# Trainium2, one core: the opening loads of a two-layer hybrid decoder trunk, in pieces of 256 KB instead of 128 KB

## The chip, the core and the metric

The kernel runs on one core of a Trainium2 chip. The core's engines run beside each other and are tied by semaphores: PE (TensorE: products of 128x128 weights with a moving operand, into PSUM), ACT (ScalarE), DVE (VectorE), POOL (GpSimd) and SP (SyncE), which here issues nearly all DMAs. The metric is the device time of one execution in microseconds (us), as the median of several runs. The profile is of one further execution.

## What is computed

Two layers of a decoder trunk on 1024 tokens of width 1024, all in float32. Cut to what matters:

```python
for l in range(DEPTH):                                # 2 layers
    h = rmsnorm(x, attn_norm[l])
    proj = h @ w_in[l]                                # split among four mixers
    y_a = mla_attention(c_q, c_kv, k_r, ...)          # latent attention
    y_b = short_gated_conv(g_b, g_c, u_conv, conv_w[l])
    y_c = multiscale_pool(u_pool, pool_w[l], pool_scale[l])
    y_d = swa_sink_attention(q_sw, k_sw, v_sw, ...)   # sliding window
    mixed = rmsnorm_per_group(stack(y_a, y_b, y_c, y_d)) * mix_norm[l]
    x = x + mixed @ w_o[l]
    h2 = rmsnorm(x, ffn_norm[l])
    gate, up = split(h2 @ w_gate_up[l])
    x = x + (silu(gate) * up) @ w_down[l]
return rmsnorm(x, final_norm)
```

## The kernel before

The tokens are the free axis, in two halves t of 512; the width is cut into eight k-tiles of 128 rows. So x is sixteen tiles of 128x512 (256 KB), held transposed in DRAM (`xT`).

A float32 product is made of three passes in a reduced format: an operand f is split into a rounded high part (one ACT instruction, L377 or, with a gain, L382) and a low part, f minus the high part (one DVE instruction, L380 or L383). `split` (L373 on) does this, `mm3` (L345) issues high by high, high by low and low by high. Each product of a weight tile with a moving tile thus stands as three rows on PE.

Before anything has landed PE runs `WARM` passes on a tile of ones (L606); what they make is not used. A float32 pass shows as two records in the profile, so WARM = 6 is twelve records.

The first work is two column groups of layer 0's input projection (the sliding-window keys and values), accumulated over the eight k-tiles in two PSUM banks, `ps_mm` and `ps_s`. Their weights come ahead of all others in four pieces `w_first` of 128x512, each for two k-tiles. Per k-tile, ACT makes the high part of the x-tile and its square for the norm, DVE the low part and the sum of squares; per weight piece there is a cast on ACT and a subtraction on DVE. A further weight, `w_in[0, 0]`, follows for the queries.

In the program before, the first k-tile is entered in halves of FIRST = 256 columns (`enter_first`, L477 on, `first_weights`, L494 on): SP loads

1. `first`: the small parameters of all layers (86 columns) and the first 256 columns of the first x-tile,
2. the first half of the first weight piece (what the first k-tile needs),
3. the other 256 columns of the first x-tile,
4. the second half of the weight piece,

and then whole tiles and pieces in the order of need. The first k-tile's products run over 256 columns each, twelve in all.

Loads, ACT, DVE, PE, POOL and SP orders are not written out by hand beyond that. The program is traced, a list scheduler (`Order`, with its own table of costs) looks for an order of all instructions on each engine, chooses buffers for it, tries it against drawn delays and imposes the best one found (`scheduled_kernel`). `behind(a, b)` adds an order between two instructions without a wait. The loads at the start are chained with it, so SP keeps their sequence. A changed program is scheduled anew from its start to its end.

At most eight of SP's loads are on their way: the ninth waits for the first to land.

After the input projection come the mixers and the output projection (in the profile until about 425 us), then the FFN (until about 1040), and the same again for layer 1 (mixers until 1425). In the FFN the products follow a scheme of sums of blocks; some sums are made ahead by DMAs into DRAM tensors `gd` and loaded from there (L1387).

Of the kernel before, what the change touches and what calls it, by code (L numbers as in the profile page):

```python
# [47 lines left out]
WARM = 6  # L48
FIRST = 256
# [80 lines left out]
def trunk_kernel(ctx: ExitStack, tc: tile.TileContext, ins, out, given=None, ends=None):  # L130
# [214 lines left out]
    def mm3(o, terms, start=True, stop=True, again=False):  # L345

        nonlocal last_mm
        n, opening = len(terms), None
        for k, (wh, wl, rh, rl) in enumerate(terms):
            for i, (w, r) in enumerate(((wh, rh), (wh, rl), (wl, rh))):  # L350
                last_mm = pe.matmul(  # L351
                    o,
                    w,
                    r,
                    start=start and k == 0 and i == 0,
                    stop=stop and k == n - 1 and i == 2,
                    skip_group_check=again,
                )
                opening = opening or last_mm
        return opening  # L360
# [10 lines left out]
    last_lo = None  # L371

    def split(hi, lo, f, gain=None, after=None):  # L373

        nonlocal last_lo
        if gain is None:
            a = act.copy(hi, f)  # L377
            if after is not None:
                behind(a, after)
            last_lo = dve.tensor_tensor(out=lo, in0=f, in1=rd(hi), op=ALU.subtract)  # L380
        else:
            a = act.activation(hi, f, AF.Copy, scale=gain)  # L382
            last_lo = dve.scalar_tensor_tensor(  # L383
                out=lo, in0=f, scalar=gain, in1=rd(hi), op0=ALU.mult, op1=ALU.subtract
            )
        return a
# [80 lines left out]
    first_cols = (slice(0, FIRST), slice(FIRST, HT))  # L467
# [9 lines left out]
    def enter_first():  # L477


        s = F.pair()  # L480
        loads.append(sp.dma_start(F.ap2(s)[:, HT - PC_ALL : HT + FIRST], ins["first"]))
# [10 lines left out]
        behind(dve.tensor_copy(par, got), lows[0])  # L492

    def first_weights(n):  # L494

        ks = slice(n * 2 * P, (n + 1) * 2 * P)
        if n == 0:
            wraw.append(F.half())
            wkv.append((R.half(), R.half()))
        f, (h, lo) = F.ap(wraw[0])[:, ks], wkv[0]  # L500
        loads.append(sp.dma_start(f, ins["w_first"][0][:, ks]))
        split(R.ap(h)[:, ks], R.ap(lo)[:, ks], f)
# [10 lines left out]
    def first_terms(i, t, k, cols):  # L513
        cs = slice(2 * (k % 2) * P + i * P, 2 * (k % 2) * P + i * P + P)
        hi, lo = (R.ap(v)[:, cs] for v in wkv[k // 2])
        return [(hi, lo, *(R.ap(v)[:, cols] for v in hh[k][t]))]
# [28 lines left out]
    for l in range(L):  # L545
# [57 lines left out]
        if l == 0:  # L603
# [3 lines left out]
            wkv, wraw, loads, lows, opened = [], [], [], [], []  # L607
            for j in range(NK // 2):
                if j == 0:
                    enter_first()  # L610
                    F.free(wraw[0])
                else:
                    wraw.append(F.half())
# [12 lines left out]
            F.free(xf[0][0] - 1)  # L626
# [27 lines left out]
            for i in range(L):  # L654
                for o, c, n in ((nsink, PC_SINK, 4), (nffn, PC_FFN, NK)):
                    d = dve.tensor_scalar(
# [6 lines left out]
                    behind(d, last_lo)  # L663
# [1665 lines left out]
def _layout(i):  # L2329
# [69 lines left out]
    a["first"] = c(np.concatenate([lay.reshape(P, -1), fin, a["xT"][0, :, :FIRST]], axis=1))  # L2399
    two = a["w_in"][0, 2:4].reshape(2, P, NK // 2, 2, P)  # L2400
    a["w_first"] = c(two.transpose(2, 1, 3, 0, 4)).reshape(NK // 2, P, HT)
# [30 lines left out]
```

## Time and profile before

| what | us |
|---|---|
| median of three runs (2028.12 to 2030.2) | 2028.17 |
| the profiled execution's own time | 2027.67 |
| its span, first to last instruction | 2025.9 |
| PE busy | 2011.1 |
| DVE busy | 1533.0 |
| ACT busy | 1026.0 |

How to read it: the span is what the profile covers; the time has some launch and end around it. The rows of a timeline give start, duration, engine, line and operation, then the tile written and those read, and the count where several like ones are merged; in brackets stands how long the engine was idle before and what released it. Rows of busy time by stretch give the stretch, its length, then PE, PEld (weight loads), DVE, ACT and POOL busy with their counts, the granted TensorE clock, the share of the DMA engines' time in use and GB/s. `PEld` lies beside PE and takes no time of its own as long as PE is busy.

### The profile page before, as it was taken

Reading aid. Unit: us, or ns where it says so; the run is one execution under the profiler, and the core shown is the slowest. Engines: PE = TensorE matmul, PEld = TensorE weight load, DVE = VectorE, ACT = ScalarE, POOL = GpSimd, SP = SyncE. Lnnn points to the kernel's source line nnn. Section 1 sums busy time; section 2 is a strip of 40 time slices with the busy share of each in tenths; the row PEclk is TensorE's granted clock in tenths of the full one; section 3 lists DMA queues with packets and bytes.
Section 4 is the critical chain, followed back from the end, with each engine's and each line's share of the span. In section 5 each row is a group of like instructions: output and inputs, shape, how many; then the busy total and the mean of one; then the engine's idle time right before and its main releaser. Section 6 shows DMA issues by size and latency. Waiting matters only on the chain.

```text
span 2025.9 us, 26686 instructions
## 1 busy us (share of the span) xinstructions
PE 2011.1 (99%) x9392; PEld 1671.5 (83%) x9392; DVE 1533.0 (76%) x2332; ACT 1026.0 (51%) x1774; POOL 570.2 (28%) x440
## 2 busy tenths in 40 slices
PE   9999999999999999999999999999999999999998
PEld 7888888888888888888888888888888888888887
DVE  8889978997677778776646898789876766775554
ACT  8457657843333335545533676677433333354343
POOL 0110000047877883000000000000687677710000
PEclk9999999999999999999999999999999999999999
DMA  6552233346767677998822134242454554487552
GB/s 206 112 105 62 72 103 110 122 150 213 208 203 204 199 209 262 385 349 290 285 71 66 48 94 130 98 154 89 164 183 166 201 172 168 163 314 250 188 178 84
DMA packets 157623, 345.90 MB, mean 171 GB/s; under 512 B 15280, under 2 KB 63024, under 8 KB 157488
## 3 DMA queue, kind: packets, MB, share of 16 engines
q1 hardware_dynamic: 150768, 326.88, 47.0%
q0 software_dynamic: 6720, 17.30, 5.2%
q8 instruction: 74, 1.21, 0.2%
q14 instruction: 61, 0.50, 0.1%
HBM read 248.71 MB, written 111.67 MB: 178 GB/s over the span
## 4 chain that ended last, share of the span: by engine, by line
PE 95%; DVE 3%; ACT 1%; DMA 1%; issue 0%; SPq 0%; DVEq 0%; ACTq 0%
PE ps_mm L351 37%; PE ps_s L351 29%; PE ps_t L351 11%; PE ps_pv L351 9%; PE ps_pv L1195 2%; PE ps_t L1183 2%; PE ps_s L1125 1%; PE ps_s L1127 1%; PE ps_s L1126 1%; PE ps_pv L797 1%; PE ps_s L719 1%; PE ps_t L785 1%; PE ps_t L437 1%; PE ps_s L996 0%; DVE u L429 0%
## 5 line engine op out<-in xcount | busy, mean ns | idle before, releaser
L351 PE MATMUL ps_mm<-u,u 128*128 128x512 f32 (+1 forms) x3415 | 837.5, 388 | 2.9 <-ACT u L377 1.9
L351 PEld LDWEIGHTS ps_mm<-u,u 128*128 128x128 f32 x3415 | 624.0, 188 | 127.4 <-ACT u L377 4.5
L380 DVE TENSOR_TENSOR u<-u,u 128x1024 fp32r<-128x1024 f32 (+4 forms) x466 | 510.1, 1115 | 180.9 <-ACT u L377 151.5
L351 PE MATMUL ps_s<-u,u 128*128 128x512 f32 (+1 forms) x2607 | 620.0, 389 | 1.0 <-ACT u L382 1.0
L377 ACT CAST u<-u 128x1024 fp32r<-128x1024 f32 (+4 forms) x466 | 393.4, 862 | 378.3 <-DMA u<-ad 75.2
L351 PEld LDWEIGHTS ps_s<-u,u 128*128 128x128 f32 x2607 | 489.5, 188 | 102.7 <-ACT u L382 1.2
L351 PE MATMUL ps_t<-u,u 128*128 128x512 f32 (+1 forms) x1080 | 245.1, 377 | 0.1
L351 PEld LDWEIGHTS ps_t<-u,u 128*128 128x128 f32 x1080 | 194.9, 188 | 38.0 <-DVE u L1412 0.4
L1192 POOL MEMSET u<- 128x128 f32 x32 | 6.1, 217 | 700.2 <-PE ps_mm L351 468.3
L351 PE MATMUL ps_pv<-u,u 128*128 128x512 f32 x792 | 190.7, 389 | 0.2 <-DVE u L1444 0.2
L351 PEld LDWEIGHTS ps_pv<-u,u 128*128 128x128 f32 x792 | 148.6, 188 | 31.5 <-DVE u L1444 0.7
L1577 POOL TENSOR_TENSOR tm<-tm,u 128x512 f32<-128x512 f32 x76 | 120.9, 1591 | 130.3 <-ACT tm L1575 130.2
L1575 ACT ACTIVATE tm<-tm 128x512 f32<-128x512 f32 x76 | 48.0, 632 | 144.1 <-DVE tm L458 144.0
L377 ACT CAST u<-ps_t 128x512 fp32r<-128x512 f32 (+3 forms) x132 | 64.4, 503 | 51.5 <-PE ps_t L1183 26.5
L380 DVE TENSOR_TENSOR u<-ps_t,u 128x512 fp32r<-128x512 f32 (+3 forms) x132 | 74.8, 581 | 15.1 <-ACT u L377 14.0
L1473 ACT COPY tm<-ps_s 128x512 f32<-128x512 f32 x62 | 36.3, 586 | 96.6 <-PE ps_s L351 92.0
L1393 POOL TENSOR_TENSOR u<-u 128x512 f32<-128x512 f32 x38 | 71.3, 1876 | 33.9 <-DVE u L380 32.7
L1655 POOL TENSOR_TENSOR u<-u,u 128x352 f32<-128x352 f32 x64 | 80.4, 1257 | 1.1
L325 POOL DMA_DIRECT2D gd<-in_w_gu x36 | 32.0, 890 | 172.8 <-PE ps_t L351 72.1
L1655 POOL TENSOR_TENSOR u<-u 128x352 f32<-128x352 f32 x64 | 74.2, 1162 | 7.7 <-DMA u<-in_w_dn 7.2
L421 ACT ACTIVATE tm<-u 128x512 f32<-128x512 f32 (+1 forms) x91 | 53.9, 599 | 43.1 <-DVE u L1839 35.6
L458 DVE TENSOR_TENSOR tm<-tm,u 128x512 f32<-128x512 f32 x76 | 70.6, 929 | 2.2
(205 smaller groups left out, 2311.0 us busy)
## 6 DMA issues: line engine op xcount, KB each, us to landing
u<-in_w_gu SPq DMA_DIRECT2D x82, 512.0 KB, 3.8
ad<-u SPq DMA_DIRECT2D x154, 256.0 KB, 2.8
u<-ad SPq DMA_DIRECT2D x70, 512.0 KB, 6.1
u<-in_w_dn SPq DMA_DIRECT2D x64, 352.0 KB, 3.5
qd<-u SPq DMA_DIRECT2D x64, 352.0 KB, 2.6
u<-in_w_in SPq DMA_DIRECT2D x43, 512.0 KB, 4.8
u<-qd SPq DMA_DIRECT2D x32, 512.0 KB, 5.6
gd<-in_w_gu POOLq DMA_DIRECT2D x30, 512.0 KB, 6.8
```

The source lines that it names most:

```text
L351: last_mm = pe.matmul(o, w, r, start=start and k == 0 and i == 0, stop=stop and k == n - 1 and i == 2, skip_group_check=again,)
L377: a = act.copy(hi, f)
L380: last_lo = dve.tensor_tensor(out=lo, in0=f, in1=rd(hi), op=ALU.subtract)
L421: act.activation(q, f, AF.Square)
L458: dve.tensor_tensor(out=o, in0=a, in1=b, op=ALU.mult)
L1183: pe.transpose(p[:, b * P : (b + 1) * P], pr[b][j // 4][:, (j % 4) * P : (j % 4 + 1) * P], ident,)
L1195: pe.matmul(py[:, c0:], v_of(j, h), R.ap(s)[:, c0:], start=j == 0 and n == 0, stop=j == nj - 1 and n == 1,)
L1393: pool.tensor_tensor(out=q4, in0=q4, in1=F.ap(self.raw[1] + 1), op=ALU.add)
L1473: act.copy(o, p)
L1575: last_silu = act.activation(g, g, AF.Silu)
L1577: pool.tensor_tensor(out=g, in0=g, in1=r, op=ALU.mult)
L1655: pool.tensor_tensor(out=o, in0=a, in1=b, op=ALU.add)
```

## The change

The first k-tile is no longer entered in halves. The weight pieces are loaded whole (128x512, 256 KB), the first of them ahead of everything; the second load is the whole first x-tile with the parameters behind it (128x598, 299 KB). `first_weights`, the tracking of the last low part and the orders that hung on it (parameter copy behind the first low part, negated parameters behind the last) are gone. WARM is 8, so sixteen records on ones instead of twelve. In DRAM `first` and `w_first` are laid out to fit.

```diff
-WARM = 6
-FIRST = 256
+WARM = 8
...
         s = F.pair()
-        loads.append(sp.dma_start(F.ap2(s)[:, HT - PC_ALL : HT + FIRST], ins["first"]))
-        xf[0][0] = s + 1
-        got, f = F.ap(s)[:, HT - PC_ALL :], F.ap(s + 1)
-        h, lo = hh[0][0] = R.half(), R.half()
-        first_weights(0)
-        for n, cols in enumerate(first_cols):
-            if n:
-                loads.append(sp.dma_start(f[:, cols], x_in[0, :, cols]))
-            split(R.ap(h)[:, cols], R.ap(lo)[:, cols], f[:, cols], got[:, PC_ATTN : PC_ATTN + 1])
-            lows.append(last_lo)
-        first_weights(1)
-        behind(dve.tensor_copy(par, got), lows[0])
...
+        loads.append(sp.dma_start(F.ap2(s)[:, : HT + PC_ALL], ins["first"]))
+        xf[0][0] = s
+        got = F.ap(s + 1)[:, :PC_ALL]
+        hh[0][0] = half_split(F.ap(s), got[:, PC_ATTN : PC_ATTN + 1])
+        dve.tensor_copy(par, got)
...
             for j in range(NK // 2):
+                wraw.append(F.half())
+                loads.append(sp.dma_start(F.ap(wraw[j]), ins["w_first"][j]))
                 if j == 0:
+                    wkv.append(half_split(F.ap(wraw[0])))
+                    F.free(wraw[0])
                     enter_first()
-                    F.free(wraw[0])
                 else:
-                    wraw.append(F.half())
-                    loads.append(sp.dma_start(F.ap(wraw[j]), ins["w_first"][j]))
                     loads.append(enter_load(0, 2 * j))
...
-                    for cols in [whole] if t or k else first_cols:
-                        for i, p in enumerate(pkv[t]):
-                            m = mm3(
-                                p[:, cols], first_terms(i, t, k, cols), k == 0 and not cols.start, k == NK - 1
-                            )
-                            if cols.start:
-                                behind(m, opened[i])
-                            elif t == k == 0:
-                                opened.append(m)
+                    for i, p in enumerate(pkv[t]):
+                        mm3(p, first_terms(i, t, k), k == 0, k == NK - 1)
...
-                    d = dve.tensor_scalar(
+                    dve.tensor_scalar(
...
-                    behind(d, last_lo)
```

What this makes of the order is seen at three places, all at the program's start. First SP, the sequence of the loads (tile written, source, partitions x columns); before:

```order
L481 DMA u_112<-in_first 128x342
L501 DMA u_115<-in_w_first 128x256
L488 DMA u_112<-in_xT 128x256
L501 DMA u_115<-in_w_first 128x256
L475 DMA u_129<-in_xT 128x512
L614 DMA u_129<-in_w_first 128x512
L475 DMA u_132<-in_xT 128x512 x2
```

and SP's loads now:

```order
L585 DMA u_114<-in_w_first 128x512
L473 DMA u_119<-in_first 128x598
L467 DMA u_125<-in_xT 128x512
L585 DMA u_125<-in_w_first 128x512
L467 DMA u_128<-in_xT 128x512 x2
```

Four loads have become two; from the second x-tile on the sequence is the same.

On ACT, at the same place, L382 is an x-tile's high part, L377 a weight's, L412 and L421 are squares; before:

```order
L382 ACTIVATE u_114<-u_112 128x256
L377 CAST u_116<-u_115 128x256
L412 ACTIVATE u_159<-u_112 128x512
L377 CAST u_116<-u_115 128x256
L382 ACTIVATE u_114<-u_112 128x256
L382 ACTIVATE u_176<-u_129,par 128x512
L421 ACTIVATE tm<-u_129 128x512
L382 ACTIVATE u_191<-u_132,par 128x512
L377 CAST u_188<-u_129 128x512
```

and ACT now (the same lines are L375, L370, L405 and L414):

```order
L370 CAST u_116<-u_114 128x512
L375 ACTIVATE u_121<-u_119 128x512
L405 ACTIVATE u_155<-u_119 128x512
L414 ACTIVATE tm<-u_125 128x512
L375 ACTIVATE u_166<-u_125,par 128x512
L375 ACTIVATE u_181<-u_128,par 128x512
L370 CAST u_178<-u_125 128x512
```

The weight now comes first, the second tile's square stands ahead of its high part, and the third x-tile (its high part is u_181, before u_191) still stands ahead of the second weight piece.

On PE the first tile's rows, and where the third tile's begin (the moving operand's high or low part stands first, the weight piece second); before:

```order
L606 MATMUL ps_pv<-tm 128x128 x6
L351 MATMUL ps_mm<-u_114,u_116 128x256
L351 MATMUL ps_s<-u_114,u_116 128x256 x2
...
L351 MATMUL ps_mm<-u_176,u_116 128x512 x2
L351 MATMUL ps_s<-u_176,u_116 128x512 x2
L351 MATMUL ps_mm<-u_191,u_188 128x512
```

and PE now:

```order
L581 MATMUL ps_pv<-tm 128x128 x8
L350 MATMUL ps_s<-u_121,u_116 128x512
L350 MATMUL ps_mm<-u_121,u_116 128x512 x3
L350 MATMUL ps_s<-u_121,u_116 128x512 x2
L350 MATMUL ps_s<-u_166,u_116 128x512
L350 MATMUL ps_mm<-u_166,u_116 128x512 x3
L350 MATMUL ps_mm<-u_181,u_178 128x512
L350 MATMUL ps_s<-u_166,u_116 128x512 x2
```

The first tile has six rows for twelve, and two of the second tile's rows (u_166) have moved behind the third tile's first one (u_181). Past the start, rows have moved against each other on all engines in the mixers of both layers; on PE hardly any have in the FFN.

More of the change, by code (lines that the diff above doesn't have):

```diff
@@ L379, in split @@
                 behind(a, after)
-            last_lo = dve.tensor_tensor(out=lo, in0=f, in1=rd(hi), op=ALU.subtract)
+            dve.tensor_tensor(out=lo, in0=f, in1=rd(hi), op=ALU.subtract)
         else:
             a = act.activation(hi, f, AF.Copy, scale=gain)
-            last_lo = dve.scalar_tensor_tensor(
+            dve.scalar_tensor_tensor(
                 out=lo, in0=f, scalar=gain, in1=rd(hi), op0=ALU.mult, op1=ALU.subtract
@@ L511, in enter_sum, with first_terms @@
         F.free(xf[k][t])
-    def first_terms(i, t, k, cols):
-        cs = slice(2 * (k % 2) * P + i * P, 2 * (k % 2) * P + i * P + P)
+    def first_terms(i, t, k):
+        cs = slice(2 * i * P + k % 2 * P, 2 * i * P + k % 2 * P + P)
         hi, lo = (R.ap(v)[:, cs] for v in wkv[k // 2])
-        return [(hi, lo, *(R.ap(v)[:, cols] for v in hh[k][t]))]
+        return [(hi, lo, R.ap(hh[k][t][0]), R.ap(hh[k][t][1]))]
     def gain(d):
@@ L606, in trunk_kernel @@
                 pe.matmul(warm[:, :P], start, start, start=True, stop=True)
[L607 removed]
+            wkv, wraw, loads = [], [], []
             for j in range(NK // 2):
+                wraw.append(F.half())
+                loads.append(sp.dma_start(F.ap(wraw[j]), ins["w_first"][j]))
                 if j == 0:
+                    wkv.append(half_split(F.ap(wraw[0])))
+                    F.free(wraw[0])
                     enter_first()
[L611 removed]
                 else:
[L613 to L614 removed]
                     loads.append(enter_load(0, 2 * j))
@@ L625, in trunk_kernel @@
                 behind(a, b)
-            F.free(xf[0][0] - 1)
+            F.free(xf[0][0] + 1)
             pkv = []
@@ L2398, in _layout @@
     fin = i["final_norm"].reshape(NK, P).T
-    a["first"] = c(np.concatenate([lay.reshape(P, -1), fin, a["xT"][0, :, :FIRST]], axis=1))
-    two = a["w_in"][0, 2:4].reshape(2, P, NK // 2, 2, P)
-    a["w_first"] = c(two.transpose(2, 1, 3, 0, 4)).reshape(NK // 2, P, HT)
+    a["first"] = c(np.concatenate([a["xT"][0, :, :HT], lay.reshape(P, -1), fin], axis=1))
+    two = a["w_in"][0, 2:4].reshape(2, P, NK // 2, 2 * P)
+    a["w_first"] = c(two.transpose(2, 1, 0, 3)).reshape(NK // 2, P, HT)
     a["rope_q"], a["rope_k"], a["const"] = _constants()
```

14 lines of the change are left out of this document (1 added, 13 removed).

## The prediction

> **What bounds the kernel now.** I read the page's busy table first, then the busy time by stretch, then the order of time of the first 13 us, and last the loads' times to landing. The table:
>
> ```profile
> span 2025.9 us, 26686 instructions
> PE 2011.1 (99%) x9392; PEld 1671.5 (83%) x9392; DVE 1533.0 (76%) x2332; ACT 1026.0 (51%) x1774; POOL 570.2 (28%) x440
> ```
>
> PE is without work for 2025.9 - 2011.1 = 14.8 us in all. The change removes no product from it: twelve of 256 columns become six of 512. So only these 14.8 us can shrink, and anything lost must be added to them. Busy time by stretch (the second column is the stretch's length, the third PE's busy time) says where they lie; the last line is the page's group of most of PE's products:
>
> ```profile
> 0.00:9.84 9.84, 6.78 (x31) 5.49 (x31) 4.11 (x10) 5.84 (x11) 0.21 (x4) 1.00 0.71 225
> 11.98:25.00 13.02, 13.02 (x57) 10.79 (x58) 12.94 (x20) 12.43 (x23) 0.00 (x0) 1.00 1.04 390
> 50.00:425.00 375.00, 373.34 (x1841) 308.81 (x1840) 333.76 (x689) 241.42 (x514) 20.01 (x35) 1.00 0.38 99
> 425.00:1040.00 615.00, 615.00 (x2715) 509.13 (x2714) 441.37 (x465) 267.46 (x353) 277.46 (x200) 1.00 0.74 245
> 1040.00:1425.00 385.00, 383.97 (x1900) 320.37 (x1899) 319.54 (x670) 242.14 (x517) 5.47 (x18) 1.00 0.29 93
> 1425.00:1990.00 565.00, 565.00 (x2522) 469.00 (x2521) 377.98 (x408) 225.02 (x302) 265.30 (x182) 1.00 0.56 191
> 2016.86:2025.90 9.04, 0.53 (x2) 0.12 (x2) 3.34 (x6) 1.53 (x4) 0.00 (x0) 0.59 0.34 116
> L351 PE MATMUL ps_mm<-u,u 128*128 128x512 f32 (+1 forms) x3415 | 837.5, 388 | 2.9 <-ACT u L377 1.9
> ```
>
> Four parts: 9.84 - 6.78 = 3.06 us in the start, 1.66 in layer 0's mixers (375 - 373.34), 1.03 in layer 1's (385 - 383.97), and 9.04 - 0.53 = 8.51 at the end, where the last tiles are normalized and stored. Both FFN stretches have none, and there 615 us hold 2715 products: one each 0.227 us. A product's own record lasts 0.388 us in the mean, the next beginning before its end, so waits under some 0.16 us don't show as idle; the 2.7 us of the mixers are what can be seen. The granted clock is 1.00 until the end, so the throttle is out of it.
>
> **The start, step by step.** In order of time (start us, us, what; in brackets the idle time before and what ended it):
>
> ```profile
> 0.74 0.39 SPq L481 DMA_DIRECT2D u<-in_first  x1
> 1.19 0.42 SPq L501 DMA_DIRECT2D u<-in_w_first  x1
> 1.05 2.93 PE L606 MATMUL ps_pv<-tm 128*128 128x128 f32 x12 [1.05 <-DVE tm L200]
> 4.13 0.55 PE L351 MATMUL ps_mm<-u,u 128*128 128x256 f32 x1
> 4.83 0.28 PE L351 MATMUL ps_mm<-u,u 128*128 128x256 f32 x1
> 6.32 0.38 PE L351 MATMUL ps_s<-u,u 128*128 128x256 f32 x1 [0.97 <-ACT u L382]
> 4.93 0.63 ACT L412 ACTIVATE u<-u 128x512 f32<-128x512 f32 x1 [0.98 <-DMA u<-in_xT]
> 6.17 0.71 ACT L382 ACTIVATE u<-u,par 128x512 fp32r<-128x512 f32 x1
> 6.79 0.61 ACT L421 ACTIVATE tm<-u 128x512 f32<-128x512 f32 x1
> 6.92 0.75 DVE L383 SCALAR_TENSOR_TENSOR u<-u,par,u 128x512 fp32r<-128x512 f32 x1
> 8.55 0.72 ACT L382 ACTIVATE u<-u,par 128x512 fp32r<-128x512 f32 x1 [1.15 <-DMA u<-in_xT]
> 9.19 0.60 ACT L377 CAST u<-u 128x512 fp32r<-128x512 f32 x1
> 9.84 0.50 PE L351 MATMUL ps_mm<-u,u 128*128 128x512 f32 x1 [0.87 <-ACT u L377]
> ```
>
> PE opens with the passes on ones, has its first product at 4.13, then waits 0.97 and 0.87 us. The point that counts is 9.84: there the products of the third k-tile begin, released by the cast of the second weight piece (9.19), which stands on ACT behind the third x-tile (8.55), which waited for its DMA. From 11.98 to 25 PE is busy throughout. So the work of the first two k-tiles (twelve products of 512 columns, 12 x 0.227 = 2.7 us) lies in a hole of 9.84 - 4.13 = 5.7 us, and when exactly they begin costs nothing until the hole is used up. **The third x-tile's landing sets the start, not the first load's.**
>
> Landings (KB each, then us from issue to landing; issue times from the rows above and the SP queue's):
>
> ```profile
> 3.55 0.91 SPq L475 DMA_DIRECT2D u<-in_xT  x2
> u<-in_first SPq DMA_DIRECT2D x1, 171.0 KB, 2.4
> u<-in_w_first SPq DMA_DIRECT2D x1, 128.0 KB, 2.2
> u<-in_xT SPq DMA_DIRECT2D x1, 256.0 KB, 3.3
> u<-in_xT SPq DMA_DIRECT2D x1, 256.0 KB, 5.0
> GB/s 0 0 0 0 0 18 82 285 324 329 202 171 188 222 246 324 352 410 362 260 239 253 259 212 205 157 225 307 341 382 362 355 382 396 389 403 417 417 389 417
> ```
>
> The first load is there at 0.74 + 2.4 = 3.14, the third x-tile at 3.55 + 5.0 = 8.55. The last row is what the DMA engines moved in slices of 0.3 us of the first 12 us. It dips from 329 to about 200 GB/s between 3.0 and 4.5, while the three 128 KB pieces pass: SP issues one load each 0.45 us (1.19 - 0.74), so 128 KB pieces can't feed more than 131 KB / 0.45 us = 290 GB/s. With pieces of 256 KB and more that limit is about 580, and this dip should go.
>
> **What the change does to it.**
> 1. *The first product comes later.* It needs the weight piece (256 KB) and the whole first tile with the parameters (299 KB), together 568,000 bytes. By the slices some 115,000 have moved at 2.4 us; the rest at 325 GB/s takes 1.4 us, so 3.8; landings here lag the bytes by 0.5 us (first load: its 175,000 bytes have passed at 2.6, landed 3.14) to 1.6 us (third x-tile: passed at 6.9 by the slices, landed 8.55). So 4.3 to 5.4; I take 4.5, near the first load's lag. Then ACT's 512-column activation, 0.72, gives PE its first product at **5.25 instead of 4.13**. Its low half is DVE's 512-column form, 0.75, so the other four products run from 6.05 to 6.95.
> 2. *Four more pass records on ones* (WARM 8 for 6): 2.93 x 8/6 = 3.9 us, from 1.05 to 4.96, before the 5.25: hidden behind the loads, even at the earliest landing (4.3 + 0.72 = 5.0). Without that cover they cost 1.0 us at most (four of the twelve records' 2.93).
> 3. *Pace.* The first product took 0.55 us, the same shape from 4.83 on 0.28, though the granted clock stands at 1.00: until 4.8, some 3.8 us after PE began, a column took twice the time. With 3.9 us of passes ahead I count all real products at 0.227. Were the first tile's six still at the slow pace, its end would be up to 6 x 0.227 = 1.4 us later, still inside the hole.
> 4. *Work off PE.* The 256-column forms and a small copy:
>
> ```profile
> 3.15 0.51 ACT L382 ACTIVATE u<-u 128x256 fp32r<-128x256 f32 x1 [1.13 <-DMA u<-in_first]
> 3.69 0.48 DVE L383 SCALAR_TENSOR_TENSOR u<-u,u 128x256 fp32r<-128x256 f32 x1 [2.43 <-ACT u L382]
> 4.09 0.20 DVE L492 COPY par<-u 128x86 f32<-128x86 f32 x1
> ```
>
>    Two halves of 256 become one of 512: ACT's 0.51 twice becomes 0.72, DVE's 0.48 twice 0.75, so each is eased by 0.2 to 0.3 us per split. Four small DVE instructions (the negated sinks and gains) move from a late place to right behind the first tile; each is bounded by the 0.20 of the parameter copy, 0.8 together, in a DVE gap from 6.0 to the second tile's activation at 6.9. If that cover were gone the second tile would be 0.8 later at most, also inside the hole.
> 5. *The third x-tile.* The same 1,354,000 bytes lie ahead of its end as before, but the dip (1.5 us at 206 instead of 325 GB/s, 180,000 bytes) is worth 0.55 us. So 7.9 for 8.55, between 8.5 (nothing gained) and 7.0 (the later dip at 157 to 260 GB/s goes as well). ACT has the activation of the second tile behind it at 6.9, so it is free. Order on ACT is unchanged here: x-tile, then weight cast; product at 7.9 + 0.64 + 0.60 + 0.05 = 9.2, not 9.84: **-0.65**.
> 6. *Two products moved.* PE's row now has two of the second tile's products behind the third tile's first one, which waits: 2 x 0.227 = **+0.45** that the hole held before.
> 7. *The rest of the program.* The list scheduler runs again on the changed program, so rows move on every engine in both mixers, though hardly in the FFN stretches of PE. Nothing in the edit asks for that; its price is bounded by the mixers' waits: below by -2.7 (1.66 + 1.03, all that is seen, gone). Above, the nearest rows are the two layers themselves, one code in two orders: they differ by 0.63, so two of them by some 1.3. I take 0 and keep -1.3 to +1.3 as the usual spread.
>
> A rule that would have item 5 otherwise stands apart: the Trainium skill (DMA: Bandwidth & Descriptors, section Anatomy of one DMA) fits a transfer, on another path of issue, as 2.0 us plus its bytes at 436 GB/s. The first load agrees (2.4 by the fit and in the row); the third x-tile doesn't (by its 1,354,000 bytes at 5.9, in the row at 8.55). What it would give is the second rival.
>
> Sum: -0.65 + 0.45 + 0 = **-0.2 us**. The profiled execution took 2027.67 us, its span 2025.9, the 1.8 between them untouched; it lies 0.5 under the median of the three runs, 2028.17. So 2027.5 by the profile, and **2028.0** as a median.
>
> **Rivals.**
> - *The change gains nothing at the third tile, and its late first product counts.* With 8.55 as before the two moved products alone give +0.45. Beyond that, ACT takes first tile, two squares and second tile in a row (0.72 + 0.63 + 0.61 + 0.72 = 2.7 us by its 512-column rows), so a first tile landing after 8.55 - 2.7 = 5.9 pushes the third one, microsecond for microsecond: at 6.5 it is +1.1, the whole of 5.25 - 4.13. For it: lags of 1.6 us were seen. Against: 5.9 would be a lag of 2.1, and the hole is 5.7 us for 2.7 us of work. 2028.6 to 2029.3, say 2029.0.
> - *Every landing is early*: the second dip goes too, third tile at 7.0, the product at 8.3, -1.55 + 0.45 = -1.1. Against: 256 KB pieces were already moving in the second dip, so their size can't be its cause. 2027.1. By the skill's fit it would be this case as well.
> - *Slower*: the hand-over to the FFN. There ACT waits for a load just ahead of PE's need,
>
> ```profile
> 422.40 1.05 ACT L377 CAST u<-u 128x1024 fp32r<-128x1024 f32 x1 [0.68 <-DMA u<-gd]
> u<-gd SPq DMA_DIRECT2D x6, 512.0 KB, 3.8
> 1412.83 0.73 PE L351 MATMUL ps_mm<-u,u 128*128 128x512 f32 x2 [0.49 <-ACT u L377]
> ```
>
>    If the new order issues one such load only when PE needs it, PE stands for landing and cast, 3.8 + 1.05 = 4.9 us: 2028.0 + 4.9 = 2032.9. It decides once the load is issued less than 4.9 us ahead; then 0.2% is passed (+4.06) if 4.1 of it is uncovered. For it: the new order moves SP's rows. Against: now ACT's lateness reaches PE there with 0.49 us at most (the same place in layer 1, last row), and the loads stand in the same sequence among themselves.
> - *The waits of the mixers go as well*: -2.7 - 1.1 = -3.8, 2024.4. It needs everything at once; even then it is under 0.2%.
>
> **How the numbers follow.** Within 0.2% (about what a measurement can tell from no change) means 2024.1 to 2032.2. Forecast 0.58, late first product 0.18, early landings 0.14, slower 0.06, all waits gone 0.04 (half of it past the bound, with the waits that don't show). So faster 0.02, slower 0.06, within 0.92. Range: rivals one and two with the spread of the mixers: 2027.1 - 1.3 = 2025.8; above 2029.3 + 1.3 = 2030.6, and as the runs of before reach 2.0 above their median (2030.2), 2030.8. Less than 2 in 10 is left out.
>
> **What would show it.** Right: the first product near 5.25, the third tile's first product near 9.2 with ACT still released there by the third x-tile's DMA, no slices near 200 GB/s between 3.0 and 4.5, mixers with 1 to 2 us without work each. Step 1 is wrong if PE begins before 4.9 or after 6; step 5 if the third tile's product is at 9.8 or later; step 7 if any mixer stretch holds over 3 us; and the whole if a gap over 1 us shows in an FFN stretch.

## The result, and the profile after

The changed kernel takes 2030.87 us in the median of 20 runs (2030.54 to 2033.25), the kernel before beside it 2028.16 (20 runs, 2027.74 to 2030.2). The ratio is 1.0014, 95% interval 1.0008 to 1.0021: slower by 2.7 us, within 0.2% as forecast, but on the wrong side of 2028.0 and just past the upper end of the range, 2030.8. The profiled execution took 2030.55 us, its span 2028.7.

The page's busy table of the changed kernel:

```profile
span 2028.7 us, 26696 instructions
PE 2013.5 (99%) x9390; PEld 1670.3 (82%) x9390; DVE 1541.1 (76%) x2330; ACT 1027.1 (51%) x1772; POOL 567.1 (28%) x440
```

PE is without work for 15.2 us, not 14.8, and its busy time has grown by 2.4 us. Four more records on ones are some 0.9 of that (3.79 us for sixteen against 2.93 for twelve); the rest I put down to waiting too short to show as a gap. So busy time alone does not find the loss; the counts of products do. Busy time by stretch in the changed kernel (stretch, its length, PE's busy time and records, then PEld, DVE, ACT, POOL, clock, DMA share and GB/s):

```profile
0.00:9.84 9.84, 8.08 (x31) 6.04 (x32) 5.30 (x14) 6.83 (x11) 0.20 (x4) 1.00 0.80 268
50.00:425.00 375.00, 373.45 (x1845) 310.40 (x1844) 334.46 (x687) 242.02 (x514) 19.81 (x34) 1.00 0.37 99
425.00:1040.00 615.00, 613.89 (x2707) 507.37 (x2706) 439.91 (x462) 266.48 (x352) 273.76 (x200) 1.00 0.74 244
740.00:780.00 40.00, 38.90 (x171) 31.54 (x170) 30.57 (x26) 13.19 (x19) 29.73 (x22) 1.00 0.57 163
1040.00:1425.00 385.00, 383.41 (x1889) 316.75 (x1888) 316.95 (x667) 242.78 (x516) 5.01 (x17) 1.00 0.29 93
1160.00:1360.00 200.00, 199.10 (x1005) 164.45 (x1004) 168.45 (x353) 137.44 (x300) 3.54 (x16) 1.00 0.34 109
```

Layer 0's FFN, which had 2715 products and no gap in 615 us, holds 2707: eight products of 0.227 us are 1.8 us. All of it lies between 740 and 780 us. Layer 1's mixers hold 1889 records for 1900.

The start, in order of time:

```profile
0.75 0.39 SPq L585 DMA_DIRECT2D u<-in_w_first  x1
1.06 3.79 PE L581 MATMUL ps_pv<-tm 128*128 128x128 f32 x16 [1.06 <-DVE tm L199]
3.43 0.62 ACT L370 CAST u<-u 128x512 fp32r<-128x512 f32 x1 [1.41 <-DMA u<-in_w_first]
4.51 0.72 ACT L375 ACTIVATE u<-u 128x512 fp32r<-128x512 f32 x1 [0.47 <-DMA u<-in_first]
5.29 0.50 PE L350 MATMUL ps_s<-u,u 128*128 128x512 f32 x1 [0.44 <-ACT u L375]
6.65 1.48 ACT L375 ACTIVATE u<-u,par 128x512 fp32r<-128x512 f32 x2
8.03 0.60 ACT L370 CAST u<-u 128x512 fp32r<-128x512 f32 x1
8.68 0.19 PEld L350 LDWEIGHTS ps_mm<-u,u 128*128 128x128 f32 x1 [0.19 <-ACT u L370]
```

and what its DMA engines moved, in slices of 0.3 us of the first 12 us:

```profile
GB/s 0 0 0 0 0 27 150 137 382 369 351 374 265 222 266 328 341 375 321 314 287 259 300 321 280 376 423 389 410 410 396 410 396 423 396 396 451 396 416 423
```

The first product stands at 5.29 (forecast 5.25). The third tile's first weights are loaded at 8.68, its product follows some 0.1 us later, at 8.77 (forecast 9.2, before 9.84). ACT takes the second and the third x-tile's activation in one row from 6.65 on, with a gap of only 0.04 us between them: the third tile landed at 7.38, against 8.53, just as ACT was done with the second. The dip in the bytes moved, from 3.6 us on, still goes down to 222 GB/s, but is shorter. In this profile the start has gained, and more than was forecast.

### The profile page after: what moved, and what is told of

It is laid out like the page before. It is cut to its first block, busy times and chain, and to the rows that moved or that the text cites. A ratio compares the mean times of both kernels' runs of the same rounds, so it can differ in the third digit from the quotient of the medians.

```text
span 2028.7 us, 26696 instructions
## 1 busy us (share of the span) xinstructions
PE 2013.5 (99%) x9390; PEld 1670.3 (82%) x9390; DVE 1541.1 (76%) x2330; ACT 1027.1 (51%) x1772; POOL 567.1 (28%) x440
## 3 DMA queue, kind: packets, MB, share of 16 engines
q8 instruction: 74, 1.21, 0.2%
## 4 chain that ended last, share of the span: by engine, by line
PE 89%; DVE 5%; ACT 1%; POOL 1%; issue 1%; DMA 1%; DVEq 0%; POOLq 0%; ACTq 0%; SPq 0%
PE ps_mm L350 34%; PE ps_s L350 27%; PE ps_t L350 11%; PE ps_pv L350 8%; PE ps_pv L1163 2%; PE ps_t L1151 2%; PE ps_s L1093 1%; DVE u L373 1%; PE ps_s L1094 1%; PE ps_s L1095 1%; PE ps_s L687 1%; PE ps_pv L765 1%; PE ps_t L753 1%; DVE u L376 1%; DVE u L1303 0%
## 5 line engine op out<-in xcount | busy, mean ns | idle before, releaser
L373 DVE TENSOR_TENSOR u<-u,u 128x1024 fp32r<-128x1024 f32 (+2 forms) x465 | 523.0, 1146 | 167.8 <-ACT u L370 133.7
L350 PE MATMUL ps_s<-u,u 128*128 128x512 f32 x2604 | 621.1, 389 | 0.9 <-ACT u L375 0.6
L370 ACT CAST u<-u 128x1024 fp32r<-128x1024 f32 (+3 forms) x465 | 392.9, 864 | 382.3 <-DMA u<-ad 77.0
L1545 POOL TENSOR_TENSOR tm<-tm,u 128x512 f32<-128x512 f32 x76 | 130.2, 1713 | 136.5 <-ACT tm L1543 136.5
L370 ACT CAST u<-ps_t 128x512 fp32r<-128x512 f32 (+3 forms) x132 | 64.3, 502 | 57.4 <-PE ps_t L1151 32.6
L373 DVE TENSOR_TENSOR u<-ps_t,u 128x512 fp32r<-128x512 f32 (+3 forms) x132 | 74.5, 580 | 18.2 <-ACT u L370 17.9
L1623 POOL TENSOR_TENSOR u<-u 128x352 f32<-128x352 f32 x64 | 79.2, 1239 | 9.8 <-DMA u<-in_w_dn 6.4
L451 DVE TENSOR_TENSOR tm<-tm,u 128x512 f32<-128x512 f32 x76 | 78.1, 1028 | 2.1
L414 ACT ACTIVATE tm<-u 128x512 f32<-128x512 f32 (+1 forms) x91 | 54.0, 599 | 42.4 <-DVE u L1807 34.1
L1361 POOL TENSOR_TENSOR u<-u 128x512 f32<-128x512 f32 x38 | 66.8, 1757 | 31.1 <-DVE u L373 31.1
L375 ACT ACTIVATE u<-u,par 128x512 fp32r<-128x512 f32 x91 | 63.6, 716 | 21.2 <-DVE u L451 12.7
```

Source lines behind the costliest of these rows:

```text
L350: last_mm = pe.matmul(o, w, r, start=start and k == 0 and i == 0, stop=stop and k == n - 1 and i == 2, skip_group_check=again,)
L414: act.activation(q, f, AF.Square)
L451: dve.tensor_tensor(out=o, in0=a, in1=b, op=ALU.mult)
L1361: pool.tensor_tensor(out=q4, in0=q4, in1=F.ap(self.raw[1] + 1), op=ALU.add)
L1545: pool.tensor_tensor(out=g, in0=g, in1=r, op=ALU.mult)
L1623: pool.tensor_tensor(out=o, in0=a, in1=b, op=ALU.add)
```

## Where the time is lost: one table for all kernels

For each kernel and stretch the time lost is the stretch's length less the sum over its products of their step (the spacing of a product's start from the next in undisturbed rows: 0.2267 us for 512 columns, elsewhere rounded to 0.227, 0.174 for 384, 0.12 for 256, 0.11 for 128 and for a record of the pass on ones). One product more or less at an edge makes 0.23 us, so small negative numbers are zeros. "Plan" (the set of orders that the scheduler makes for the whole program) is explained in the fourth group of experiments. All kernels of the study, in us:

| kernel | start, records on ones | orders of the rest | median | 0 to 25 | 25 to 425 | 740 to 780 | 1160 to 1360 |
|---|---|---|---|---|---|---|---|
| before | old, 12 | stretched plan | 2028.16 | 6.14 | 8.53 | -0.13 | 3.02 |
| changed | new, 16 | unstretched plan | 2030.87 | 5.10 | 7.62 | 1.69 | 5.65 |
| new_start_old_rest | new, 16 | those of before | 2027.76 | 4.42 | 9.44 | 0.10 | 3.25 |
| new_start_12_records | new, 12 | those of before | 2027.27 | 5.54 | 7.62 | -0.13 | 3.28 |
| old_start_16_records | old, 16 | those of before | 2028.19 | 5.70 | 8.53 | -0.13 | 3.25 |
| old_start_new_rest | old, 12 | those of the change | 2032.63 | 6.82 | 7.62 | 2.14 | 5.65 |
| old_start_seed_2 | old, 12 | stretched | 2027.20 | 6.14 | 8.76 | 0.10 | 3.25 |
| old_start_seed_3 | old, 12 | stretched | 2028.57 | 6.14 | 9.21 | 0.10 | 3.25 |
| new_start_seed_2 | new, 16 | stretched | 2027.29 | 4.88 | 8.08 | 0.10 | 3.04 |
| new_start_seed_3 | new, 16 | unstretched | 2031.15 | 4.88 | 7.62 | 1.69 | 5.88 |
| old_start_unstretched_plan | old, 12 | unstretched | 2032.71 | 6.82 | 8.08 | 2.37 | 5.42 |
| new_start_stretched_plan | new, 16 | stretched | 2028.98 | 4.42 | 9.89 | 0.10 | 3.02 |
| new_start_12_stretched_plan | new, 12 | stretched, drawn with 12 | 2026.02 | 5.77 | 7.62 | 0.10 | 3.04 |
| sixteen_on_plan_of_twelve | new, 16 | the same orders | 2025.45 | 4.20 | 8.53 | 0.10 | 3.05 |
| twelve_again | new, 12 | the same kernel again | 2026.71 | 4.86 | 7.41 | 0.10 | 3.07 |
| pool_sums_later | new, 16 | the change's, two moves | 2030.30 | 4.88 | 8.77 | 1.01 | 5.87 |
| ffn_pool_and_dve | new, 16 | the change's, three moves | 2028.99 | 5.33 | 8.32 | -0.13 | 5.64 |
| pe_sums_later | new, 16 | the change's, two moves | 2032.54 | 5.56 | 7.64 | 1.69 | 6.55 |
| dve_sum_earlier | new, 16 | the change's, one move | 2031.80 | 4.88 | 7.86 | 2.14 | 6.32 |

From before to the change: the start -0.68 (5.10 - 6.14, and 0.44 back for the four more records, which count as products here, less 0.08, as twelve products of 256 columns count 1.44 and six of 512 count 1.36), layer 0's mixers -0.91, the FFN between 740 and 780 us +1.82, layer 1 between 1160 and 1360 us +2.63, all else about zero: together +2.9, the spans differ by 2.8.

Each row is one profile. The changed kernel and the four with moves in its orders are alike on every engine up to 740 us, and yet their first column runs from 4.88 to 5.56 and their second from 7.62 to 8.77. So neither the start's -0.68 nor layer 0's -0.91 can be told from this scatter by one profile. The last two columns differ by far more than they scatter: on the stretched plan they hold -0.13 to 0.10 and 3.02 to 3.28, on the unstretched one, without moves, 1.69 to 2.37 and 5.42 to 5.88.

## The experiments

**1. The start and the rest taken apart.** The theory: the start has gained 0.7 us, as argued, and the loss comes from the new order of everything behind it. The rival: the start itself causes it, by its loads or its shift in time. Two kernels cross them. Each takes the instructions of the opening (pass records, the first load and weight piece, the first tile's parts and products) from one version, and the orders and buffers of all others, on every engine, from the other's plan (the edit in short):

```diff
-    return trace(*best[1], best[2])[0]
+    rest, own = planned(REST), planned(START)
+    return trace(START, *rest[1], merged(rest[2], own[2]))[0]
```

Two more leave before's orders in place and change only the count of pass records (`WARM` 6 or 8).

> The new loads, pieces and pass records of the start, with the orders and buffers of the kernel before for every instruction behind it. Theory (the loss is the new order of the rest): the third tile's first product near 8.7 us, PE ahead by 0.7 us from then on, and nothing given back in the FFN or in layer 1: 2028.16 - 0.7 = 2027.5 us, within 2026.9 to 2028.2. Rival (the loss comes from the start itself, by its loads and its earlier clock of work, whatever order follows): as the changed kernel, 2030.9, at least 2030.

> The loads, halves and twelve pass records of before, with the orders and buffers of the changed kernel for every instruction behind them. Theory: the loss without the gain, 2030.87 + 0.7 = 2031.6 us, with 104 products instead of 112 between 750 and 775 us again. Rival (the start does it): as before, 2028.2.

> As the first of these four, but twelve pass records on ones, not sixteen. Theory: the records lie beside the loads and change nothing, since the third tile's first product waits for its tile and ACT: as the first one within 0.2 us; the first products may run at half pace again (0.40 to 0.55 us each instead of 0.28) and still end before the third tile's. Rival (the sixteen records are worth something by themselves): slower than the first one by 0.5 us or more.

> The kernel before in every order, with sixteen pass records instead of twelve. Theory: they end at 4.96 us for 3.98, so the first product comes 0.8 us later than its 4.13, inside the hole ahead of the third tile at 9.84: 2028.2 within 0.2 us. Rival (the records shift the time of the whole): 2029 or more.

Measured, beside 2028.15 for the kernel before: 2027.76 (ratio 0.9997, interval 0.9988 to 1.0006), 2032.63 (1.0022, 1.0013 to 1.0031), 2027.27 (0.9995, 0.9986 to 1.0004) and 2028.19 (1.0, 0.999 to 1.0009). The orders of the rest cost 3.1 us behind the new start (2030.87 - 2027.76) and 4.5 behind the old one; the loss follows them, between 740 and 780 as between 1160 and 1360 us (table). The new start by itself is worth 0.4 us, with twelve records 0.9, each inside its interval of no change, so a gain is likely and not shown. Sixteen records in the old start cost nothing. Two expectations were missed in size: the old start with the new orders is 1.0 above its 2031.6, and twelve records are 0.5 faster than sixteen where 0.2 at most was expected. The rival, the start by itself, is out.

**2. The FFN's loss.** The change leaves PE's sequence in this stretch as it was. But PE waits twice there now, as its order of time shows:

```profile
756.84 2.88 PE L350 MATMUL ps_mm<-u,u 128*128 128x512 f32 x12
760.06 5.76 PE L350 MATMUL ps_s<-u,u 128*128 128x512 f32 x24 [0.34 <-DVE tm L1742]
768.38 2.88 PE L350 MATMUL ps_s<-u,u 128*128 128x512 f32 x12
772.03 3.01 PE L350 MATMUL ps_mm<-u,u 128*128 128x512 f32 x12 [0.77 <-DVE tm L1453]
```

Twelve products take 12 x 0.227 = 2.72 us, so the second row could have begun at 759.56 and the fourth at 771.10: 0.50 and 0.93 us lost, with 0.11 behind each. Each time DVE reads a bank too late that PE wants to fill. What could hold DVE up is this, in the changed kernel (L373 is the low part of a weight pair, 1024 columns):

```profile
751.77 4.81 DVE L373 TENSOR_TENSOR u<-u,u 128x1024 fp32r<-128x1024 f32 x1
...
752.00 1.35 POOL L1623 TENSOR_TENSOR u<-u,u 128x352 f32<-128x352 f32 x1
752.91 1.68 POOL L1545 TENSOR_TENSOR tm<-tm,u 128x512 f32<-128x512 f32 x1
754.16 1.32 POOL L1623 TENSOR_TENSOR u<-u,u 128x352 f32<-128x352 f32 x1
756.65 2.21 POOL L1361 TENSOR_TENSOR u<-u 128x512 f32<-128x512 f32 x1 [1.17 <-DVE u L373]
```

while before has, at the same place:

```profile
752.89 1.38 DVE L380 TENSOR_TENSOR u<-u,u 128x1024 fp32r<-128x1024 f32 x1 [0.79 <-PE ps_s L351]
754.74 1.77 DVE L380 TENSOR_TENSOR u<-u,u 128x1024 fp32r<-128x1024 f32 x1 [0.47 <-ACT u L377]
```

The low part takes 4.81 us instead of some 1.2. It ends at 756.58, 1.10 us after POOL's unbroken row of three sums (754.16 + 1.32 = 755.48): nearly its whole length alone, so beside that row it hardly got on. Then POOL in turn waits 1.17 us for it. The Trainium skill (SBUF — State Buffer, section Who interferes with whom) says that a DVE instruction with two inputs in SBUF contends with a GpSimd instruction that reads there, and that the loser fully blocks; the trace agrees, 4.81 against 1.22. By these rows DVE began 0.23 us ahead of the first of the three sums and lost all the same. Moving two sums on POOL breaks the row:

```diff
 gd<-in_w_gu
-L1623 u<-u,u 128x352
 L1545 tm<-tm,u 128x512
-L1623 u<-u,u 128x352
 L1361 u<-u 128x512
+L1623 u<-u,u 128x352
+L1623 u<-u,u 128x352
```

> The changed kernel with one move on POOL in layer 0's FFN, near 751 us: behind the weight load stand the activation's product and the fourth gate sum, and only then the two 352-column sums of the down weights that stood before and between them; every other order is the changed kernel's. Theory (PE's loss of 1.7 us between 740 and 780 us comes from DVE's 1024-column low part at 751.8, which took 4.81 us beside POOL's unbroken row of sums, against 1.22 alone): that low part takes under 3 us, and the stretch from 740 to 780 us loses under 0.6 us instead of 1.68: about 2029.6 us, 2029.2 to 2030.2. Rival (the loss comes from DVE's or PE's own order there, and the long low part is only a symptom): 2030.9, same within 0.3.

Measured 2030.30 (1.0012, 1.0003 to 1.0021). DVE's order of time, and then PE's, in this run (its lines are numbered otherwise: L383 is the low part, L1518 the reading of the bank):

```profile
752.66 1.21 DVE L383 TENSOR_TENSOR u<-u,u 128x1024 fp32r<-128x1024 f32 x1
...
760.41 5.60 PE L355 MATMUL ps_s<-u,u 128*128 128x512 f32 x24
765.85 2.88 PE L355 MATMUL ps_t<-u,u 128*128 128x512 f32 x12
768.57 2.88 PE L355 MATMUL ps_s<-u,u 128*128 128x512 f32 x12
772.38 3.01 PE L355 MATMUL ps_mm<-u,u 128*128 128x512 f32 x12 [0.93 <-DVE tm L1518]
```

The low part is back at 1.21 and the first wait is gone, but the second has stayed: the stretch loses 1.01, not the under 0.6 expected. The time is 0.1 above what was expected, and its ratio to before, 1.0012, can't be told from the changed kernel's 1.0014. So the long low part was less than half of the story (0.68 of the 1.69 lost). For the second wait, the instruction that PE waited for stands behind a subtraction and a sum of 512 columns on DVE, the sum taking 1.78 us there instead of the 0.68 of its shape. The next kernel keeps the move on POOL and makes one on DVE:

```diff
 L373 u<-u,u 128x1024
+L1453 tm<-ps_t,tm 128x512
 L1255 u<-u,u 128x512
 L1556 u<-u,u 128x512
-L1453 tm<-ps_t,tm 128x512
```

> The changed kernel with the move on POOL of the run before, and one on DVE: the reading of the sums bank that PE waited for at 772.03 us stands ahead of the two sums of 512 columns that it stood behind (0.68 and 1.77 us there). Theory (layer 0's FFN lost its 1.7 us in two places, each an instruction in a place where PE has to wait for it): both waits are gone, the stretch from 740 to 780 us loses under 0.4 us, and the time is that of the run before less 1.1: 2029.2 us, 2028.8 to 2029.8. Rival (DVE is behind as a whole there, and the wait moves on): 2030.3 within 0.4, with a wait of 0.5 us or more on PE between 772 and 790 us.

Measured 2028.99 (1.0005, 0.9997 to 1.0014), as expected. Its stretch is full again:

```profile
740.00:780.00 40.00, 40.00 (x178) 33.10 (x178) 26.68 (x27) 12.98 (x18) 29.65 (x22) 1.00 0.56 163
```

The FFN's 1.8 us are settled: three instructions in other places on two engines that are busy 28% and 76% of the time, and the waits are gone, with 1.88 us in the medians (2030.87 - 2028.99).

**3. Layer 1's mixers.** There the changed kernel's only wait on PE over 0.1 us that shows between 1160 and 1360 us is a pair of products on ones (for a norm), whose bank DVE has yet to read:

```profile
1227.55 0.70 PE L430 MATMUL ps_t<-u,ones_r 128*128 128x512 f32 x2 [0.72 <-DVE tm L442]
```

By the steps 0.97 us are lost at that place, 0.48 at a like one at 1193.70, 0.35 at 1223.38. Two kernels move the parties: PE's pair six products later and one product at 1193.70 five later, or DVE's reading 1.1 us earlier.

```diff
-PE: L430 ps_t<-u,ones_r x2
 PE: L350 ps_mm<-u,vhi / vlo x6
+PE: L430 ps_t<-u,ones_r x2
...
+DVE: L442 tm<-ps_t,tm 128x512
 DVE: L1098 sm<-ps_s 128x1
 DVE: L1025 u<-ps_mm,u 128x256
-DVE: L442 tm<-ps_t,tm 128x512
```

> The changed kernel with two moves on PE in layer 1's mixers: the pair of products on ones that waited for DVE at 1227.55 us stands six products later, the one that waited at 1193.70 us five later; every other order is the changed kernel's. Theory (of layer 1's loss of 2.4 us, 1.4 to 1.8 are these waits behind DVE, because the new order has DVE's part too close ahead of them): PE finds work in their place, and the stretch from 1160 to 1360 us loses about 4.1 us instead of 5.6: 2029.4 us, 2028.9 to 2030.1. Rival (DVE and ACT are behind as a whole there, so that the wait only moves to a later product): 2030.9, within 0.4.

> The changed kernel with one move on DVE in layer 1's mixers: the reading of the sums bank that PE waited for at 1227.55 us stands 1.1 us earlier, ahead of a row maximum and a low part of 256 columns; its input is there at 1226.08. Theory (DVE as a whole is behind from 1221.7 us on, after waiting for PE's product): PE's wait at 1227.55 falls from 0.97 to about 0.3, but products behind it that need the two delayed pieces take up half or all of it: 2030.2 to 2031.0. Rival (only this one place costs): 2030.2 or less, with nothing new behind.

Measured 2032.54 (1.0021, 1.0012 to 1.0029) and 2031.80 (1.0018, 1.0009 to 1.0027): both worse than the changed kernel, and both above what theory and rival had given. The stretch loses 6.55 and 6.32 us, not less than 5.65. The wait has gone to the next products in either, to the very ones put in its place or behind it, and in the first a further one has come up at 1209.71, 0.69 by the steps (L1090 is DVE's low part of the queries; the first row is of the move on PE, the second of that on DVE):

```profile
1229.28 0.70 PE L355 MATMUL ps_mm<-u,vhi 128*128 128x512 f32 x2 [1.07 <-DVE u L1090]
```

```profile
1229.24 0.70 PE L355 MATMUL ps_mm<-u,vhi 128*128 128x512 f32 x2 [1.15 <-DVE u L1090]
```

The theory of single late instructions has failed in the first run. The wait only moved, as its rival said, but the rival's time, 2030.9 within 0.4, was missed too. In the second run the wait at the pair fell as expected (0.20 by the steps), but what came behind took back more than the gain, not half or all of it. Both fit a DVE that as a whole is behind PE near 1225 us in this order; no run has put it ahead there with the other orders held, so that cause is not shown.

**4. Why the rest came out worse.** The first idea was luck: the scheduler improves its order with random draws, so another seed would give another time.

```diff
-        draw = random.Random(1)
+        draw = random.Random(2)
```

> The changed kernel, its scheduler's random draws begun from another seed: all orders behind the start are planned anew by the same rules. Theory (the loss is the luck of one order): it lands anywhere between 2026 and 2032 us, and its losses lie in other stretches than 740 to 780 and 1160 to 1360 us. Rival (the new start by itself leads the planner to worse orders): 2030.5 or more, with losses in the same two stretches.

> The kernel before, its scheduler begun from another seed. Theory (the time of the kernel before is one draw of the same spread): it differs from 2028.2 by 0.5 to 3 us in either direction. Rival (before's order is no matter of luck): 2028.2 within 0.3 us.

> The changed kernel with a third seed for its scheduler. Theory (each planning is a draw with a spread of some 1.5 us, and the changed kernel's is a bad one): 2026.5 to 2030 us. Rival (the start costs by itself): 2030.5 or more.

> The kernel before with a third seed for its scheduler. Theory (a draw of the same spread): 2026.5 to 2031 us. Rival (before's rules give 2027 to 2028.3 whatever the seed): within that.

Measured 2027.29, 2027.20, 2031.15 and 2028.57. The third is outside what I expected, and the table says why the idea was too simple: its losses are those of the changed kernel, stretch by stretch, those of the other three are those of the kernel before. In the two stretches there is no cloud of orders but two families. The scheduler's code has two as well: it makes one plan with its costs as they are and one with the costs of DVE and ACT stretched by 1.03, and imposes the one that its own model puts lower.

```diff
-SLOW = (1.0, 1.03)
+SLOW = (1.03,)
```

Left only one of the two, it gives the changed kernel's orders row for row from the unstretched plan, and those of the kernel before from the stretched one. Three runs give each start the other plan:

> The changed kernel, whose scheduler is left only the second of its two plans, the one made with the costs of DVE and ACT stretched by 1.03. (By its own model the scheduler took the unstretched plan for the changed kernel, 2012.0 against 2012.6, and the stretched one for the kernel before, 2012.5 against 2013.2.) Theory (the change flipped the choice between two plans, and the unstretched one is the slower on the chip by some 3.5 us): no long low part near 751 us, POOL's order as in the kernel before, the stretches 740 to 780 and 1160 to 1360 us losing under 0.1 and 3.5 us: 2027.4 us, 2026.7 to 2028.2. Rival (the new start costs in either plan): 2029 or more.

> The kernel before, whose scheduler is left only the first of its two plans, with the costs as they are. Theory (the choice of the plan decides, not the start): it loses as the changed kernel does, 1.5 to 2.3 us between 740 and 780 us and 5 to 6.5 between 1160 and 1360 us, and takes 2031.6 us, 2030.8 to 2033. Rival (the unstretched plan is bad only behind the new start): 2028.2 within 0.5.

> The changed kernel with twelve pass records on ones and the stretched plan alone. Theory (the records are hidden behind the loads, the plan decides): 2027.3 us, 2026.6 to 2028.2. Rival (the four more records matter): 0.5 us or more from the first of these three.

Measured 2028.98 (1.0003, 0.9995 to 1.0012), 2032.71 (1.0023, 1.0013 to 1.0032) and 2026.02 (0.9991, 0.9982 to 1.0). Stretches of the first two, the new start with the stretched plan:

```profile
740.00:780.00 40.00, 40.00 (x178) 33.17 (x177) 26.85 (x29) 14.15 (x20) 29.27 (x21) 1.00 0.62 176
1160.00:1360.00 200.00, 200.00 (x1014) 167.53 (x1013) 173.43 (x362) 137.88 (x303) 3.17 (x16) 1.00 0.34 111
```

and the old start with the unstretched one:

```profile
740.00:780.00 40.00, 38.27 (x168) 31.04 (x167) 31.64 (x26) 12.88 (x18) 29.88 (x22) 1.00 0.55 153
1160.00:1360.00 200.00, 199.10 (x1005) 164.68 (x1004) 169.28 (x356) 137.22 (x300) 3.55 (x16) 1.00 0.33 107
```

with DVE's low part there, in its order of time:

```profile
754.13 4.81 DVE L380 TENSOR_TENSOR u<-u,u 128x1024 fp32r<-128x1024 f32 x1
```

The losses have changed places with the plan. The old start loses even the same 4.81 us on DVE. The time of the first run, though, is 0.8 above my range and 1.2 above the transplant with the same start (2027.76), and at the edge of the rival's (2029 or more): its layer 0 mixers lose 9.89 us, the most of all. The third run is 0.6 below its range, and 3.0 from the first, as its rival had it. So whether the sixteen records or that draw of the plan did it was open. The last two put sixteen records on the very orders of the twelve, and time the twelve again:

> The kernel of the run with twelve pass records and the stretched plan (2026.02 us), every order the same, with four more pass records. Theory (the records are hidden; the 2028.98 of the stretched plan with sixteen came from its other draw in layer 0's mixers): 2026.0 us within 0.5. Rival (the four records cost by themselves): 2027 or more, up to 2029.

> The kernel with the large pieces, twelve pass records and the stretched plan once more, beside the run with sixteen on the same chip: 2026.0 us within 0.4, faster than the kernel before by 1.5 to 2.5 us. Rival (its first time was luck): 2027.3 or more.

Measured 2025.45 (0.9986, 0.9977 to 0.9994) and 2026.71 (0.9991, 0.9982 to 1.0) beside 2028.30. Both lie just outside what was expected, the first 0.05 below 2025.5, the second 0.3 above 2026.4. Sixteen records are faster than twelve here and were slower in group 1, so no cost of theirs shows. With sixteen records in both, 2028.98 against 2025.45 is the draw within the stretched plan; their intervals don't meet. Where the 3.5 us lie is shown in part: 1.36 of them in layer 0's mixers, where the scatter is 1.1, and 1.14 in a stretch that the table leaves out, 1360 to 1425 us (1.98 lost against 0.84). The first of the two beats both kernels: the change as it was made, on a plan drawn for twelve records, is 2.85 us faster than the kernel before.

## Why the prediction went wrong

- **What bounds it, and the start (steps 1 to 6): right in the main, on the cautious side.** First product 5.29 for 5.25. The pass records ended at 4.85, 0.44 before it: hidden, and twelve or sixteen make no steady difference (twelve 0.5 us faster in group 1, 1.3 slower in the last pair). What remains until 25 us is 0.68 us of gain in this profile; the orders of before under the new start give 0.4 at the end.
- **The third tile (step 5): right in kind, the size and the reason less so.** Its product came at 8.77, 1.07 us earlier, not 0.65: between the forecast (9.2) and my second rival ("every landing is early", 8.3). The landing still sets the start, as the prediction had it, though ACT is now free only 0.04 us ahead of it: in the five kernels that are alike up to 740 us the third tile landed at 7.20, 7.28, 7.38, 7.66 and 7.81 us, and the start lost 4.88, 4.88, 5.10, 5.33 and 5.56. Step 5's own figures give 8.0 and -0.55, not 7.9 and -0.65, a slip of 0.1 us. Its reason, that the dip is 128 KB pieces at SP's pace, held at most in part: with whole pieces the slices from 3.6 to 4.5 us still show 265, 222 and 266 GB/s, so what else makes the dip stays open.
- **Step 7 failed.** It reads: "Nothing in the edit asks for that; its price is bounded by the mixers' waits ... I take 0 and keep -1.3 to +1.3 as the usual spread." Measured is +3.5: -0.91 in layer 0's mixers, +1.82 in its FFN, +2.63 in layer 1. The first of these is within the scatter of profiles, the other two are not. Two things were wrong in the step. It took the two layers of one program for two draws of an order, but both come from the same plan; a changed program can be given another plan, and here was. And it let the FFN out because PE's rows hardly move there, while DVE's and POOL's did, and PE waits for them. "Hardly in the FFN stretches of PE" was true and beside the point.
- **The slower rival named the wrong place.** PE does not wait for a late `gd` load at the hand-over. The slower side came through the same door (a new order), but as DVE behind POOL and behind its own order in the FFN, and as DVE late for PE in layer 1's mixers.
- **The signs set down beforehand did their work.** A gap over 1 us in an FFN stretch was to make the whole wrong: 615 - 613.89 = 1.11. The mixers' stretches kept under 3 us of visible idle, 375 - 373.45 and 385 - 383.41, and yet layer 1 lost 2.6: that sign was too blunt, counts of products would have been sharp.
- **What stays open.** Which part of the unstretched plan puts DVE behind in layer 1's mixers, and why draws of the stretched plan differ by up to 3.5 us, was not settled; of the 7.41 to 9.89 us in layer 0's mixers, some 1.1 can be scatter. That the scheduler's model prefers the unstretched plan behind the new start follows from its own figures (2012.0 against 2012.6); that it does so because the model does not see a 4.81 us low part was not tried.

## What to carry to other kernels

Where a scheduler orders the whole program, an edit of ten lines can move rows everywhere: if it keeps several plans, ask first which of them the changed program will get, and hold the orders fixed (transplant them) before judging the edit itself. Here the edit by itself was worth some 0.4 to 0.9 us, not told from nothing, the orders of the other plan 3.1 and 4.5 us, and measuring several plans gave the fastest kernel. In an FFN with PE 100% busy, compare the orders of the engines that free its buffers, and count products per stretch: the 0.11 us lost behind each wait above shows no idle time at all.

## What was not expected of the hardware

A DVE low part of 1024 columns takes 1.22 us when POOL does no sum beside it (187 such instructions of 290 in the changed kernel, 1.19 to 1.23), 1.72 in the mean beside POOL, and 4.81 or 4.82 us at one place in six of the kernels, each time beside three POOL sums without a break. It is no chance slowdown: the same instruction in the same order repeats it to 0.02 us.

Nor is it peculiar to the change. The kernel before has such a row too, where the low part takes 4.15 us:

```profile
676.79 4.15 DVE L380 TENSOR_TENSOR u<-u,u 128x1024 fp32r<-128x1024 f32 x1 [0.21 <-PE ps_s L351]
...
676.74 0.97 POOL L1655 TENSOR_TENSOR u<-u,u 128x352 f32<-128x352 f32 x1
677.64 1.31 POOL L1577 TENSOR_TENSOR tm<-tm,u 128x512 f32<-128x512 f32 x1
678.89 0.95 POOL L1655 TENSOR_TENSOR u<-u,u 128x352 f32<-128x352 f32 x1
```

It ends at 680.94, 1.10 us after the last sum (679.84), as in the changed kernel: in both the end of POOL's row sets the low part's end. And PE loses nothing there; its products keep their step from 670 to 700 us. So a long low part is no loss by itself; in the changed kernel the reading of a bank that PE needed stood close behind it.
